# Another order of the prompt's query tiles, and a second buffer for the compression's chunk pairs

## The chip, the cores and the metric

One Trainium2 chip, one of its cores. The metric is the device time of one call in microseconds (us). Within one call the engines of a core run their own instruction streams side by side: PE (TensorE, matrix products), DVE (VectorE), ACT (ScalarE), POOL (GpSimd), and SP, which issues most of the transfers.

## The reference

One inference step of one layer of a hybrid decoder, for a prompt of 1024 tokens and 64 sample tokens (8 sequences of 8). The layer is a half feed-forward block, then a mixer in which attention and a Mamba-2 scan work side by side, then a second half feed-forward block. The change touches the attention alone:

```python
def nsa_mixer(q, q_pos, full_cmp, full_sel, o_win, gates, prm, slopes, sel_qb):
    kc = compress(full_cmp[:, :, 0], ...)          # 32-token blocks, stride 16, through a small MLP
    vc = compress(full_cmp[:, :, 1], ...)
    o_cmp, p_cmp = cmp_attention(q, q_pos, kc, vc, slopes)
    idx = select_blocks(p_cmp, q_pos, n_sel_blocks)
    o_sel = sel_attention(q, q_pos, idx, ...)
    g = jax.nn.sigmoid(gates)...
    return g[:, :, 0] * o_cmp + g[:, :, 1] * o_sel + g[:, :, 2] * o_win
```

For the prompt every query of tile t (128 queries) sees the keys of tiles 0 to t in the selected branch, the last 512 tokens in the window branch, and the compressed keys. For each of the 8 sample sequences a cache of 2048 tokens has to be compressed first, then its queries go through the same three branches.

## The kernel before

The kernel is one long program for one core, and a planner puts it in order: each engine gets a fixed list of instructions, made by simulating the program ahead of time. Whatever comes earlier in the program has precedence where several instructions are ready, an instruction is ready when its inputs are there and a buffer is free for its output, and a tile that is laid where older tiles were waits for the last use of those it overlaps.

The stage around the change is the prompt's attention. `for qi, qt in enumerate(KN["qt"])` (L1480) goes through the eight query tiles in the order of the tuple `qt` in the table `KN` (L37). Ahead of tile number qi it calls `compress_sample` as often as `cs[qi]` says, 3, 0, 2, 1, 1, 1, 0, 0 times, so that the eight sequences' compressions are in the program among the first six tiles. At qi 6 it also calls `mamba_setup`.

A query tile is worked off in two head groups of four heads. For each group, and for the selected (br 0) and the window branch (br 1): four heads' scores (L1549 to L1554: a matmul, a second one for the rest of the split, and masks), the maximum (DVE, L1559 to L1563), the exponential (ACT, L1565), sums and reciprocals (DVE, L1570 to L1572), and the multiplication of the four heads' probabilities by these (`scale`, L1576, on the engine that `KN["pb"][qi]` names letter by letter: a is ACT, L262, p is POOL, L264, v is DVE, L266). Then every 128 keys are one unit: four transposes into `pT` (L1587), one copy to `pt` (ACT and DVE in turn), and a matmul into `o` (L1596). Tile t has t+1 units of the selected branch, at most 5 of the window branch and one of the compressed keys in each group: 3 units for tile 0, 5, 7, 9, 11, 12, 13 and 14 for tiles 1 to 7. Between the scores of one head and its units nothing but these steps is needed; the next head, group or tile fills the waiting.

`compress_sample` (L1428) loads one sequence with an indirect transfer (`chk`, one buffer, L1430) and goes through it in eight chunk pairs: POOL and ACT each copy half a pair into `chp` (L1434), PE transposes it into `cT` (L1441, one bank, which the second product `c` of L1469 and L1472 shares), ACT makes `th` (L254), DVE makes `tl` (L1446), and 12 matmuls add to `cA` (L1462 to L1464). After four pairs come the activation `cxh` and the second product.

Once the attention's pools are closed, the program goes on with `sample_attention` and `mamba`. The first starts with a setup: some 15 index and constant tiles on POOL (`pi`, `hsel`, `G`, `E`, `bc`, `iw`, `tri`, `QS`, L1630 to L1722) and some 40 small instructions on DVE on them (L1633 to L1717, the greatest `bsel`, L1674). The pools of the new stage lie in the memory of the closed ones: those of `mamba`, with the chunk's tiles `xbc` that SP loads at L1255, grow from the left over the attention's keys, and those of `sample_attention` from the right over the attention's own tiles and then the compression's. Of a Mamba chunk the first steps are the transposes `xs_ps` (L1260), the DVE products `xdt` and `xde` (L1264, L1265) and the matmuls `ar` (L1282).

Of the kernel before, what the change touches and what calls it, by code (L numbers as in the profile page):

```python
# [9 lines left out]
F32 = mybir.dt.float32  # L10
# [7 lines left out]
P = 128  # L18
# [15 lines left out]
PAST = 2048  # L34
B0AT = (3, 5, 7, 9)
EARLY = {(0, 0): (0, 128), (1, 0): (640,), (0, 1): (), (1, 1): (768,)}
KN = {'Bt': 'a', 'cb': 'a', 'de': 'vv', 'ea': 'pp', 'st': 'p', 'hT': 'v', 'xm': 'p', 'yz': 'v', 'ysq': 'v', 'kT': 'aa', 'sPT': 'v', 'S': 'vv', 'ce': 'p', 'cm': 'p', 'pcT': 'v', 'msk': 'a', 'osb': 'av', 'q': 'sspss', 'pb': ['apppaapp', 'apppappp', 'apppappp', 'apvpappp', 'apppapvp', 'appvappp', 'vpvvvpvv', 'pvvvvvvv'], 'ph': ['aavaaa', 'aaaaaa', 'aaaaaa', 'aaaava', 'aaaaaa', 'aaaaaa', 'vavaaa', 'avaaaa'], 'pc': 'p', 'ob': 'aa', 'QA': 'aapv', 'QB': 'pv', 'chp': 'ap', 'th': 'aa', 'qt': (2, 7, 6, 5, 4, 3, 1, 0), 'cs': [3, 0, 2, 1, 1, 1, 0, 0], 'mix': [0, 0, 0, 0, 0, 0, 0, 0, 0]}  # L37
SLOPES = [2.0 ** -(h + 1) for h in range(NH)]


def f32(ap):
    return ap.bitcast(F32)
# [37 lines left out]
def hybrid_step(ctx: ExitStack, tc: tile.TileContext, *aps):  # L80
# [93 lines left out]
    def bankx(name):  # L174
        return PS.tile([P, 512], F32, name=name, tag="X", bufs=4)
# [17 lines left out]
    q = bankx("vec_ps")  # L193
# [669 lines left out]
    with pool("cv", bufs=2) as K:  # L863
# [40 lines left out]
        for group in [(0, 1)] + [(i,) for i in range(2, 8)]:  # L904
# [4 lines left out]
            if group[0] == 0:  # L909
                q = side("st_ps")  # L910
# [5 lines left out]
        for i in range(4):  # L916
            w = wcols(W, w_in, 1304 + P * i)
            zt = K.tile([P, T], F32, name="zt", tag="acc")
            for t0, n in WCHUNKS:
                q = bank("z")  # L920
# [5 lines left out]
        for z in range(2):  # L926
            q = side("cv_ps")
# [11 lines left out]
        for t0, n in WCHUNKS:  # L939
            q = bank("gd")  # L940
            dense(q, w, t0, n)
            nc.vector.tensor_tensor(gdT[:, t0:t0 + n], q[:32, :n], rms[:32, t0:t0 + n], op=OP.mult)
        q = side("gd_ps")
# [203 lines left out]
    for i in range(4):  # L1147
        w = wcols(W, w_in, P * i)
        for t0, n in WCHUNKS:
            q = bank("q")  # L1150
# [90 lines left out]
    def mamba(K, dt, dA, U, Us, Bof, bm, mU, mUs, nacs, dend, cdec, dsk):  # L1241
# [7 lines left out]
        for c in range(9):  # L1249
# [4 lines left out]
            xbc = K.tile([P, 8, P], F32, name="xbc")  # L1254
            QUEUES[KN["q"][0]].dma_start(xbc[:, :, :L], xbcD[:, :, ts].rearrange("i p t -> p i t"))  # L1255
            za = K.tile([P, 4, P], F32, name="za")
            QUEUES[KN["q"][1]].dma_start(za[:, :, :L], zD[:, :, ts].rearrange("i p t -> p i t"))
            q = b1("xs_ps")
# [10 lines left out]
            Bt = K.tile([P, 256], F32, name="Bt")  # L1269
            copy(KN["Bt"], Bt[:L], q[:L, :256])  # L1270
            cbp = b1("cb")
# [3 lines left out]
            cb = K.tile([P, 2, P], F32, name="cb")  # L1275
            copy(KN["cb"], cb[:L, :, :L], cbp[:L, :256].rearrange("p (g l) -> p g l", g=2)[:, :, :L])
            yp = b1("y")
            for g in range(2):
# [10 lines left out]
                for i in range(4):  # L1289
                    nc.scalar.activation(de[:L, i, :L], arv[:L, i, :L], AF.Exp,  # L1290
                                         bias=nacs[:L, c, 4 * g + i:4 * g + i + 1])
                sub(KN["de"][g], de[:L, :, :L], de[:L, :, :L], cb[:L, g:g + 1, :L].to_broadcast([L, 4, L]), OP.mult)
                sub(KN["ea"][g], ea[:, :, :L], ea[:, :, :L], xbc[:, 6 + g:7 + g, :L].to_broadcast([P, 4, L]), OP.mult)
                for i in range(4):
# [101 lines left out]
    CK = Ds.enter_context(pool("cmp", bufs=2))  # L1396
    PSC = Ds.enter_context(pool("cmp_ps", bufs=1, space=PSUM))
    with pool("att", bufs=2) as K, pool("att_ps2", bufs=3, space=PSUM) as PS2, \
# [29 lines left out]
        def compress_sample(b):  # L1428
            chk = CK.tile([P, 16, 2, 2, 64], F32, name="chk", bufs=1)
            nc.gpsimd.indirect_dma_start(  # L1430
                out=chk.rearrange("p s k g d -> p (s k g d)"), out_offset=None, in_=ch_cmp,
                in_offset=bass.IndirectOffsetOnAxis(ap=idx[:, b:b + 1], axis=0))
            def pairs(kv, jj):
                chp = CK.tile([P, 2, 2, 2, 64], F32, name="chp", bufs=1)  # L1434
                for g in range(2):
                    copy(KN["chp"][g], chp[:, :, g], chk[:, 4 * jj:4 * jj + 4, kv, g, :].rearrange(
                        "p (j r) d -> p j r d", r=2))
                q = b1("cT")
                for u in range(2):
                    for g in range(2):  # L1440
                        nc.tensor.transpose(q[:, P * (2 * u + g):P * (2 * u + g) + P],  # L1441
                                            chp[:, u, g].rearrange("p r d -> p (r d)"), ident)
                sv = q.rearrange("p (u c) -> p u c", u=2)
                th, tl = tpad[jj % 2]
                copy(KN["th"][jj % 2], th[:, :, :256], sv)
                nc.vector.tensor_tensor(tl[:, :, :256], sv, f32(th[:, :, :256]), op=OP.subtract)  # L1446

            steps = [(kv, jj) for kv in range(2) for jj in range(4)]
            pairs(*steps[0])
            for kv in range(2):  # L1450
                ab = PSC.tile([P, 2, P], F32, name="cA")
                for jj in range(4):
                    if (kv, jj) != steps[-1]:
                        pairs(*steps[4 * kv + jj + 1])
                    th, tl = tpad[jj % 2]
                    for u in range(2):
                        j = 2 * jj + u
                        for z in range(2):
                            wh, wl = w1h[:, kv, 8 * z + j], w1l[:, kv, 8 * z + j]
                            first = j == 0 and z == 0  # L1460
                            mh, ml = (x[:, u, z:z + 256].rearrange("p (g c) -> p g c", g=2) for x in (th, tl))
                            nc.tensor.matmul(ab, wh, mh, start=first, stop=False, skip_group_check=True)  # L1462
                            nc.tensor.matmul(ab, wl, mh, start=False, stop=False, skip_group_check=True)  # L1463
                            nc.tensor.matmul(ab, wh, ml, start=False, stop=(j == 7 and z == 1), skip_group_check=True)  # L1464
                hs = cmp_hidden(CK, ab[:, :, :127], None, kv, 127)
                q = b1("c2")
                for g in range(2):
                    if kv == 0:
                        nc.tensor.matmul(q[64 * g:64 * g + 64, :127], w2[:, 0], hs[:, g, :127],  # L1469
                                         start=True, stop=True)  # L1470
                    else:
                        nc.tensor.matmul(q[:127, 64 * g:64 * g + 64], hs[:, g, :127], w2[:, 1],  # L1472
                                         start=True, stop=True)
                if kv == 0:
                    nc.vector.tensor_copy(kcTs[:, b, :127], q[:, :127])
                else:
                    nc.vector.tensor_copy(vcs[:127, b, :], q[:127, :P])

        sequences = iter(range(8))
        for qi, qt in enumerate(KN["qt"]):  # L1480
# [5 lines left out]
            for g in range(2):  # L1486
                QA, QB = K.tile([P, 4, P], F32R, name="QA", bufs=2), QBq[g]
# [15 lines left out]
            for h in range(NH):  # L1503
                o = s[:, 64 * h:64 * h + 64]
                QA, QB = QAs[h // 4][:, h % 4], QBq[h // 4][:97, h % 4]
# [7 lines left out]
            pc = K.tile([P, NH, 64], F32, name="pc", bufs=1)  # L1513
# [12 lines left out]
            for g in range(2):  # L1526
                PT = {}
                for br in range(2):
# [6 lines left out]
                    for hh_ in range(4):  # L1535
                        pb = K.tile([P, 1024 if br == 0 else 640], F32, name=f"pb{br}", bufs=(5, 6)[br])
                        pbs.append(pb)
                        st, parts = 0, []
# [35 lines left out]
                    for hh_ in range(4):  # L1574
                        h, pb = 4 * g + hh_, pbs[hh_]
# [26 lines left out]
                ob = K.tile([P, 2, P], F32, name="ob", bufs=1)  # L1602
# [610 lines left out]
```

## Time and profile before

| | us |
|---|---|
| median of 3 runs | 2546.06 |
| lowest and highest of the 3 | 2540.13, 2546.14 |
| the profiled execution, its time | 2543.46 |
| its span, first to last instruction | 2541.8 |
| PE, DVE, ACT, POOL busy | 2449.2, 1751.7, 1092.3, 459.5 |

Times in the trace count from the start of the span. The engines' rows tell when an instruction began and how long it took; what stands in square brackets behind a row is how long the engine had been idle before, and what ended that. The two feed-forward blocks fill the span up to about 750 us and from about 1800 us on; the prompt's attention lies between about 1066 and 1485 us, and `sample_attention` and `mamba` run from there to about 1700 us.

### The profile page before, as it was taken

To read this page: it belongs to the slowest core of one execution; us is meant where nothing else is said; L and a number is where in the kernel's file an instruction comes from. 1 tells how busy PE (TensorE), PEld (TensorE's weight loads), DVE (VectorE), ACT (ScalarE), POOL (GpSimd) and SP (SyncE) were. 2 spreads that over 40 slices of the span, in tenths; PEclk is the share of its full clock that TensorE was granted. 3 is DMA by queue.
4 is the path that set the end of the run, shared out by engine and by line. 5 is a ranking of instruction groups with operands and counts; after the bars stand their busy time and mean duration, and the time that the engine had idled before them with its cause. 6 is when DMAs were issued, how large, how long until landed. Compare 5 with 4: busy or idle time off the path is not lost.

```text
span 2541.8 us, 48016 instructions
## 1 busy us (share of the span) xinstructions
PE 2449.2 (96%) x19111; PEld 2246.8 (88%) x19111; DVE 1751.7 (69%) x3601; ACT 1092.3 (43%) x2411; POOL 459.5 (18%) x545
## 2 busy tenths in 40 slices
PE   6999999999999999999999988999999999999998
PEld 6999999999999999867767755678999999999998
DVE  6767676677777546366667777656967676768776
ACT  7544444441143223166667644333544444443113
POOL 0000000011134213443334354431000000001110
PEclk9999999999999999999999989979999999999999
DMA  4334343598653223220010043543234444459654
GB/s 165 123 125 161 125 160 129 177 338 297 229 185 97 84 67 94 77 99 34 34 67 34 34 146 120 181 148 106 83 112 142 155 146 144 154 186 374 252 207 150
DMA packets 213563, 365.07 MB, mean 144 GB/s; under 512 B 17501, under 2 KB 130825, under 8 KB 211932
## 3 DMA queue, kind: packets, MB, share of 16 engines
q1 hardware_dynamic: 194408, 305.10, 34.8%
q0 software_dynamic: 7600, 38.59, 4.2%
q10 hardware_dynamic: 11332, 18.33, 2.1%
q8 instruction: 150, 2.46, 0.4%
q14 instruction: 73, 0.60, 0.1%
HBM read 246.39 MB, written 119.71 MB: 144 GB/s over the span
## 4 chain that ended last, share of the span: by engine, by line
PE 85%; DVE 8%; DMA 3%; ACT 3%; issue 1%; POOL 1%; SPq 0%; ACTq 0%; DVEq 0%; POOLq 0%
PE gY L352 6%; PE gY L353 6%; PE gY L351 6%; PE dq L609 6%; PE dq L608 5%; PE dq L610 5%; PE gX L352 5%; PE gX L353 5%; PE gX L351 5%; PE o L1596 3%; PE pT L1587 3%; PE s L1549 1%; PE cA L1462 1%; PE cA L1464 1%; PE cA L1463 1%
## 5 line engine op out<-in xcount | busy, mean ns | idle before, releaser
L609 PE MATMUL dq<-db,da 128*128 128x256 f32 (+1 forms) x1232 | 353.6, 288 | 0.3 <-DVE da L257 0.3
L610 PE MATMUL dq<-db,da 128*128 128x256 f32 (+1 forms) x1232 | 353.2, 288 | 0.0
L608 PE MATMUL dq<-db,da 128*128 128x256 f32 (+1 forms) x1232 | 349.6, 288 | 3.1 <-DMA db<-GD 1.9
L617 DVE TENSOR_TENSOR xT<-xT,dq 128x256 f32<-128x256 f32 (+1 forms) x456 | 187.1, 434 | 88.5 <-PE dq L610 86.8
L257 POOL TENSOR_TENSOR ds<-dw 128x512 f32<-128x512 f32 x22 | 29.0, 1318 | 1198.9 <-DMA dw<-in_ffn_wd_dram 515.6
L608 PEld LDWEIGHTS dq<-db,da 128*128 128x128 f32 x1232 | 230.4, 189 | 3.9 <-DVE xT L254 2.1
L610 PEld LDWEIGHTS dq<-db,da 128*128 128x128 f32 x1232 | 233.0, 189 | 0.0
L609 PEld LDWEIGHTS dq<-db,da 128*128 128x128 f32 x1232 | 232.0, 188 | 0.6 <-DVE da L257 0.5
L254 ACT CAST whi<-ws 128x512 fp32r<-128x512 f32 x156 | 96.5, 623 | 211.2 <-PE gY L353 145.2
L257 DVE TENSOR_TENSOR wlo<-raw,whi 128x512 fp32r<-128x512 f32 x164 | 113.8, 699 | 79.8 <-ACT whi L254 79.6
L254 ACT CAST da<-ds 128x512 fp32r<-128x512 f32 x88 | 52.7, 624 | 239.3 <-PE dq L610 93.4
L254 ACT CAST whi<-raw 128x512 fp32r<-128x512 f32 x176 | 109.0, 626 | 82.0 <-DMA raw<-in_w_out_dram 33.3
L257 DVE TENSOR_TENSOR wlo<-ws,whi 128x512 fp32r<-128x512 f32 x156 | 106.9, 689 | 42.0 <-ACT whi L254 39.2
L1565 ACT ACTIVATE pb<-s,mx 128x256 f32<-128x256 f32 (+3 forms) x192 | 105.2, 553 | 49.5 <-DVE mx L1563 33.0
L1587 PEld LDWEIGHTS pT<-ident,pb 128*128 128x128 f32 x528 | 59.4, 143 | 49.0 <-issue 41.5
L351 PE MATMUL gX<-B6h,whi 128*128 128x256 f32 (+1 forms) x320 | 91.4, 286 | 1.8 <-ACT Cc L358 1.8
L351 PE MATMUL gY<-B3h,whi 128*128 128x256 f32 (+1 forms) x320 | 91.5, 287 | 1.4 <-ACT whi L254 1.4
L352 PE MATMUL gX<-B6h,wlo 128*128 128x256 f32 (+1 forms) x320 | 91.8, 287 | 0.5 <-DVE wlo L257 0.5
L352 PE MATMUL gY<-B3h,wlo 128*128 128x256 f32 (+1 forms) x320 | 91.7, 287 | 0.2 <-DVE wlo L257 0.2
L352 PE MATMUL gY<-B2h,wlo 128*128 128x256 f32 (+1 forms) x320 | 91.8, 287 | 0.0
L352 PE MATMUL gX<-B7h,wlo 128*128 128x256 f32 (+1 forms) x320 | 91.7, 286 | 0.0
L351 PE MATMUL gX<-B7h,whi 128*128 128x256 f32 (+1 forms) x320 | 91.6, 286 | 0.0
(689 smaller groups left out, 8574.3 us busy)
## 6 DMA issues: line engine op xcount, KB each, us to landing
db<-GD SPq DMA_DIRECT2D x42, 1632.0 KB
GD<-Cc SPq DMA_DIRECT2D x154, 272.0 KB
GD<-his SPq DMA_DIRECT2D x84, 272.0 KB
raw<-in_ffn_wg_dram SPq DMA_DIRECT2D x22, 1024.0 KB
raw<-in_ffn_wu_dram SPq DMA_DIRECT2D x22, 1024.0 KB
dw<-in_ffn_wd_dram SPq DMA_DIRECT2D x44, 512.0 KB
GD<-hp SPq DMA_DIRECT2D x70, 272.0 KB
db<-GD SPq DMA_DIRECT2D x14, 1088.0 KB
```

Source lines behind the costliest of these rows:

```text
L254: return nc.scalar.copy(out, src) if eng == "a" else ENGINES[eng].tensor_copy(out, src)
L257: ENGINES[eng].tensor_tensor(out, x, y, op=op)
L351: nc.tensor.matmul(q, ah[:, k], b_, start=first, stop=False, skip_group_check=True)
L352: nc.tensor.matmul(q, al[:, k], b_, start=False, stop=False, skip_group_check=True)
L353: nc.tensor.matmul(q, ah[:, k], c_, start=False, stop=(k == 3), skip_group_check=True)
L608: nc.tensor.matmul(q, x, bh[:, u, o], start=first, stop=False, skip_group_check=True)
L609: nc.tensor.matmul(q, y, bh[:, u, o], start=False, stop=False, skip_group_check=True)
L610: nc.tensor.matmul(q, x, bl[:, u, o], start=False, stop=(u == np_ - 1), skip_group_check=True)
L617: nc.vector.tensor_tensor(x, x, q, op=OP.subtract if i == 4 else OP.add)
L1565: nc.scalar.activation(pb[:, st:st + pn], s, AF.Exp, bias=mx[:, 0:1], accum_out=part[:, hh_, i:i + 1])
L1587: nc.tensor.transpose(tq_[:kn, P * hh_:P * hh_ + P], src, ident)
L1596: mm = nc.tensor.matmul(O[64 * u:64 * u + 64], v_, p_, start=(ui < 2), skip_group_check=True, stop=(ui - len(held) + 1 + u >= len(units) - 2))
```

## The change

The tuple `qt` becomes 2, 7, 6, 0, 5, 1, 4, 3: the two smallest tiles move from the end to places four and six, and the last two tiles are 4 and 3. The lists of `pb` move with their tiles, so that each tile's probabilities are multiplied on the same engines as before, up to the letters' place. `cs` stays as it is, by position. The buffer `chp` of the compression has two slots in place of one; with that the pool of the attention's own tiles, which lies behind it, starts 2 KB per partition higher.

```diff
-KN = {... 'pb': ['apppaapp', 'apppappp', 'apppappp', 'apvpappp', 'apppapvp', 'appvappp', 'vpvvvpvv', 'pvvvvvvv'], ...
-      'qt': (2, 7, 6, 5, 4, 3, 1, 0), 'cs': [3, 0, 2, 1, 1, 1, 0, 0], ...}
+KN = {... 'pb': ['apppaapp', 'apppappp', 'apppappp', 'pvvvvvvv', 'apvpappp', 'vpvvvpvv', 'apppapvp', 'appvappp'], ...
+      'qt': (2, 7, 6, 0, 5, 1, 4, 3), 'cs': [3, 0, 2, 1, 1, 1, 0, 0], ...}
...
             def pairs(kv, jj):
-                chp = CK.tile([P, 2, 2, 2, 64], F32, name="chp", bufs=1)
+                chp = CK.tile([P, 2, 2, 2, 64], F32, name="chp", bufs=2)
```

## Rows read from the trace of the kernel before

**Rows 1.** The page's chain that ended last, its shares by engine.

```profile
PE 85%; DVE 8%; DMA 3%; ACT 3%; issue 1%; POOL 1%; SPq 0%; ACTq 0%; DVEq 0%; POOLq 0%
```

**Rows 2.** Busy time of the engines in stretches of the span: from A to B, its length, then busy us (and instructions) of PE, PE's weight loads, DVE, ACT and POOL, the granted clock of PE, the DMA engines' share, GB/s.

```profile
1102.00:1474.00 372.00, 366.07 (x2517) 267.54 (x2515) 246.34 (x587) 247.66 (x667) 140.61 (x211) 1.00 0.11 41
1474.00:1492.00 18.00, 9.88 (x31) 4.92 (x31) 17.12 (x70) 2.98 (x8) 15.92 (x17) 0.61 0.92 306
...
1440.00:1474.00 34.00, 34.00 (x255) 26.40 (x253) 25.91 (x79) 22.48 (x76) 9.84 (x22) 1.00 0.00 1
```

**Rows 3.** PE's instructions in order of time around the end of the attention: start, us, engine, line, what, count, idle time before.

```profile
1470.04 0.28 PE L1464 MATMUL cA<-tl,w1h 128*128 128x256 f32 x1
...
1472.10 1.07 PE L1596 MATMUL o<-pt,VAc 64*64 64x512 f32 x2
...
1473.77 0.23 PE L1554 MATMUL s<-mdiag,identb 128*128 128x128 bf16 x1
...
1477.57 0.33 PE L1587 MATMUL pT<-ident,pb 128*128 128x128 f32 x1 [3.13 <-DVE pb L266]
...
1481.31 1.97 PE L1596 MATMUL o<-pt,VA 128*64 128x512 f32 x4 [1.70 <-DVE pt L254]
1483.22 1.97 PE L1596 MATMUL o<-pt,VAc 64*64 64x512 f32 x2
1485.11 1.11 PE L1260 MATMUL xs_ps<-ident,xbc 128*128 128x128 f32 x4
...
1491.64 2.08 PE L1282 MATMUL ar<-U,dA 128*128 128x128 f32 x8 [3.28 <-DVE xde L1265]
```

**Rows 4.** The chain that ended last, from 1469 to 1499 us: start, us, what.

```profile
1475.43 0.05 DVE ti L1633
...
1477.45 1.63 DVE pb L266 x3
...
1480.66 0.60 DVE pt L254
...
1483.82 2.29 DVE bsel L1674
...
1488.88 0.42 DVE qT L1607
...
1490.38 0.60 DVE xdt L1264
1490.98 0.61 DVE xde L1265
```

**Rows 5.** POOL's instructions in order of time: a tile's multiplications, the last of the attention, and the first of the setup.

```profile
1414.44 3.04 POOL L264 TENSOR_TENSOR pb<-pb,sm 128x512 f32<-128x512 f32 x3 [1.17 <-DVE sm L1572]
...
1470.27 0.40 POOL L264 TENSOR_TENSOR pb<-pb,sm 128x128 f32<-128x128 f32 x1 [5.90 <-DVE sm L1572]
1470.63 0.17 POOL L1630 IOTA pi<- 128x1 int32 x1
```

**Rows 6.** SP's issues in order of time.

```profile
1473.96 0.39 SPq L1255 DMA_DIRECT2D xbc<-xbcD  x1
```

**Rows 7.** The timelines of PE, ACT, DVE and POOL, their lines of the compression: two pairs that follow one another closely, and two between which POOL's copy came late.

```profile
1194.63 0.61 PE L1441 MATMUL cT<-ident,chp 128*128 128x128 f32 x4
1195.75 0.41 ACT L254 COPY chp<-chk 128x256 f32<-128x256 f32 x1
1195.89 0.69 DVE L1446 TENSOR_TENSOR tl<-cT,th 128x512 fp32r<-128x512 f32 x1 [0.28 <-ACT th L254]
1197.32 0.61 PE L1441 MATMUL cT<-ident,chp 128*128 128x128 f32 x4
...
1261.80 0.60 PE L1441 MATMUL cT<-ident,chp 128*128 128x128 f32 x4
1265.44 0.39 POOL L254 COPY chp<-chk 128x256 f32<-128x256 f32 x1
1270.14 0.60 PE L1441 MATMUL cT<-ident,chp 128*128 128x128 f32 x4
```

**Rows 8.** The first transposes of the first and of the last sequence, from PE's timeline.

```profile
1102.86 0.60 PE L1441 MATMUL cT<-ident,chp 128*128 128x128 f32 x4
...
1428.06 0.60 PE L1441 MATMUL cT<-ident,chp 128*128 128x128 f32 x4
```

**Rows 9.** Groups of instructions by line and shape in the attention: line, engine, operation, out<-in, shapes, count, then busy us and mean ns of one, then idle time before and its releasers. The last row is from 1475 to 1497 us, the others from 1100 us on.

```profile
L1565 ACT ACTIVATE pb<-s,mx 128x512 f32<-128x512 f32 x40 | 27.3, 686 | 7.0 <-DVE mx L1563 4.5 <-DVE mx L1559 1.7 <-PE pT L1587 0.6
L1559 DVE TENSOR_REDUCE mx<-s 128x1 f32<-128x512 f32 x16 | 10.5, 685 | 1.1 <-PE s L1554 1.0
L266 DVE TENSOR_SCALAR pb<-pb,sm 128x128 f32<-128x128 f32 x14 | 4.8, 396 | 0.1
L266 DVE TENSOR_SCALAR pb<-pb,sm 128x128 f32<-128x128 f32 x4 | 2.0, 564 | 0.0
```

**Rows 10.** Busy time in stretches early in the attention, before the first transposes of the compression; columns as in rows 2.

```profile
1075.00:1080.00 5.00, 4.57 (x14) 2.94 (x14) 3.35 (x8) 4.34 (x12) 5.00 (x5) 0.50 1.09 410
1080.00:1085.00 5.00, 3.71 (x17) 2.21 (x15) 4.27 (x11) 3.86 (x13) 4.74 (x10) 0.79 0.99 342
1085.00:1090.00 5.00, 4.49 (x17) 2.52 (x17) 1.94 (x5) 3.48 (x10) 3.80 (x5) 0.55 0.60 166
1090.00:1095.00 5.00, 4.84 (x27) 3.24 (x26) 2.70 (x7) 2.72 (x8) 2.45 (x5) 0.77 0.76 324
```

More of the change, by code (lines that the diff above doesn't have):

```diff
@@ L36 @@
 EARLY = {(0, 0): (0, 128), (1, 0): (640,), (0, 1): (), (1, 1): (768,)}
-KN = {'Bt': 'a', 'cb': 'a', 'de': 'vv', 'ea': 'pp', 'st': 'p', 'hT': 'v', 'xm': 'p', 'yz': 'v', 'ysq': 'v', 'kT': 'aa', 'sPT': 'v', 'S': 'vv', 'ce': 'p', 'cm': 'p', 'pcT': 'v', 'msk': 'a', 'osb': 'av', 'q': 'sspss', 'pb': ['apppaapp', 'apppappp', 'apppappp', 'apvpappp', 'apppapvp', 'appvappp', 'vpvvvpvv', 'pvvvvvvv'], 'ph': ['aavaaa', 'aaaaaa', 'aaaaaa', 'aaaava', 'aaaaaa', 'aaaaaa', 'vavaaa', 'avaaaa'], 'pc': 'p', 'ob': 'aa', 'QA': 'aapv', 'QB': 'pv', 'chp': 'ap', 'th': 'aa', 'qt': (2, 7, 6, 5, 4, 3, 1, 0), 'cs': [3, 0, 2, 1, 1, 1, 0, 0], 'mix': [0, 0, 0, 0, 0, 0, 0, 0, 0]}
+KN = {'Bt': 'a', 'cb': 'a', 'de': 'vv', 'ea': 'pp', 'st': 'p', 'hT': 'v', 'xm': 'p', 'yz': 'v', 'ysq': 'v', 'kT': 'aa', 'sPT': 'v', 'S': 'vv', 'ce': 'p', 'cm': 'p', 'pcT': 'v', 'msk': 'a', 'osb': 'av', 'q': 'sspss', 'pb': ['apppaapp', 'apppappp', 'apppappp', 'pvvvvvvv', 'apvpappp', 'vpvvvpvv', 'apppapvp', 'appvappp'], 'ph': ['aavaaa', 'aaaaaa', 'aaaaaa', 'aaaava', 'aaaaaa', 'aaaaaa', 'vavaaa', 'avaaaa'], 'pc': 'p', 'ob': 'aa', 'QA': 'aapv', 'QB': 'pv', 'chp': 'ap', 'th': 'aa', 'qt': (2, 7, 6, 0, 5, 1, 4, 3), 'cs': [3, 0, 2, 1, 1, 1, 0, 0], 'mix': [0, 0, 0, 0, 0, 0, 0, 0, 0]}
 SLOPES = [2.0 ** -(h + 1) for h in range(NH)]
```

## The prediction

> **What bounds the kernel now.** I read the page's chain first: it goes through PE for 85% of the span and through DVE for 8% [rows 1], so a change can only save where PE stands still, runs at half its clock, or where the chain leaves it. Then I cut the attention into stretches. From 1102 to 1474 us PE is busy for 366.07 of 372 us at full clock [rows 2]: 5.9 us to be had there in all, and whatever is put in another order inside it keeps its sum. From 1474 to 1492 us the picture turns over: PE 9.88 of 18 us, at a mean clock of 0.61, and DVE 17.12 of 18 [rows 2]. The loss is in these 18 us, and the change bears on what runs there.
>
> The third view, PE's timeline, shows what they consist of. The last scores of tile 0 end at about 1474.0 us; then PE waits 3.13 us for DVE's multiplications and 1.70 us for a copy, does its last four and two matmuls into `o` in 1.97 us each where the group before took 1.07, transposes Mamba's first chunk at 1485.11 and waits 3.28 us for `xde` before `ar` at 1491.64 [rows 3]. The fourth view, the chain, says why: from 1475.43 to 1491.64 us, 16.2 us, it lies nearly all on DVE. Of that the attention and Mamba own `pb` 1.63, `pt` 0.60, `qT` 0.42, `xdt` 0.60 and `xde` 0.61 [rows 4], 3.9 us together; the other 12.3 us, with `bsel` alone 2.29 [rows 4], are the setup of the sample attention and small steps. The setup stands in front of the attention's last steps and of Mamba's first.
>
> Why doesn't it run sooner? POOL makes its first index tile at 1470.63 us, directly behind its last multiplication; before that multiplication POOL had been idle for 5.90 us and did not take it [rows 5]. PE issues the compression's last product at 1470.04 us [rows 3]. By the sizes in the code the setup's tiles lie over the compression's weights and buffers, and I take the end of the compression for what lets them in. So a second chain matters: the compression of eight sequences, whose first transposes are at 1102.86 us for the first and at 1428.06 for the last [rows 8], 325.2/7 = 46.5 us for each. It ends only 3.7 us before the last scores do (1473.77 less 1470.04, rows 3), which is why the setup has nothing to hide behind.
>
> **Part 1: the second `chp` buffer.** It adds no instruction. With one slot the copies for a pair wait for the transposes of the pair before, with two they may be done one pair ahead, and the gather of the next sequence, which waits for the last copies, may be issued that much sooner. What it saves depends on what spaces the pairs. In a close pair, transposes at 1194.63 and 1197.32 us, ACT's copy is there at 1196.16 and `tl` leaves the bank `cT` at 1196.58 [rows 7]: there the bank decides, and the second buffer saves nothing. In a wide one, transposes at 1261.80 us, POOL's copy starts at 1265.44, 3.0 us after they end, behind other POOL work [rows 7]; there up to 3.0 us go. By my count of the timeline about ten pairs of 64 are like that, mostly less late. Ends: nothing, and ten times 3.0, 30 us, for all eight sequences; I take 12, nearer to the close pair, which is the usual one. PE is full meanwhile, so these microseconds are no gain by themselves: the compression's share of PE comes sooner and the tiles' later.
>
> **Part 2: the order.** The same 148 units (2 groups of 3, 5, 7, 9, 11, 12, 13 and 14) are worked off; only the place of tiles 0 and 1 and the two last tiles change. Tiles 0 and 1 with their short chains go to where PE has compression and tiles 5 and 4 to fill with; their waits (3.13 and 1.70 us now) are covered there by the score matmuls of the next tile. If that cover failed they would stand inside the full stretch, as much as now, 4.8 us. I cost this at nothing, with ends of 4.8 us lost and, since 5.9 us are idle there now, 3 gained.
>
> The end is now tile 3's. *Old end:* 3.13 + 1.70 us idle, and half clock: two `o` groups at 1.97 in place of 1.07, 1.8 us, and some 0.5 on the transposes; 7.1 us. *New end,* from tile 3's last score: maximum 0.69 and exponential 0.69 [rows 9], about 0.4 of small steps, then POOL's three multiplications of 512 columns, 3.04 us in that tile now [rows 5], together 4.8 us before the window branch's units can start. To cover that PE has, at best, the four units of the selected branch: a unit is four transposes, at most 0.61 us as those of the compression [rows 7], I take 0.5 behind one another, and about 0.25 of the 1.07 us of four `o` [rows 3]: 0.75 us, four of them 3.0. So PE idles 1.8 us at the least and 4.8 if those units are done already. Behind it come five units at 0.75, where only the last copy and pair, about 0.6 us, is bare. New end: 2.4 to 5.4, and up to 2.3 more if the clock falls as it does now; I take 5.2. Part 2 saves 7.1 − 5.2 = **1.9 us**, between −0.6 and 4.7.
>
> SP is moved too: it can issue `xbc` when the last scores have read the keys, 1473.96 us now, right behind the score at 1473.77 [rows 3, 6]. With tile 3 that issue has more matmuls behind it than with tile 0, so the load stays hidden. `mamba_setup` goes from tile 1 to tile 4, further from the end; it is hidden by PE's fullness in both places.
>
> **Part 3: the setup.** With the compression ending 12 us sooner, and the last scores about 3 us sooner (tile 3 leaves more PE work behind them), its lead over the last scores grows from 3.7 to about 13 us. In that lead DVE has its idle share: 1 − 25.91/34 = 24% in the last 34 us, 34% over the whole attention [rows 2]. So 3.1 to 4.4 us of DVE's setup leave the 12.3 on the chain; I take **4.0**. Ends: 0 (no lead), and 9 (the lead is long; what remains of the 18 us is about the 9.2 us that the new end needs anyway: 4.8, five units at 0.75 and 0.6).
>
> **Sum.** −1.9 − 4.0 = −5.9 us, against the profiled execution 2543.46 − 5.9 = 2537.6. That execution lies 2.6 us under the median of the three runs; carried to the median, 2546.06 − 5.9 = **2540.2 us**. What follows the attention is moved sooner as a whole; I allow 3 us either way for where its transfers and clock falls come to lie.
>
> **Rivals.** *The setup is hidden whole.* The compression ends 25 us or more ahead (30 saved, the upper end of part 1). Then 9 us go from the setup and 3 from the end: 2546.1 − 12 = 2534. For it: 9 of the 12.3 us have no other reason to be there. Against: DVE's idle share of 24% fills slowly.
>
> *The buffer does nothing.* If `cT` and its sharing with `c` space nearly all pairs, as in the close one [rows 7], the compression ends where it does and the setup stays behind it; only the end's 1.9 us are left: 2544.
>
> *POOL and DVE hold each other up.* Four multiplications of 128 columns on DVE took 0.564 us each beside the busy POOL of the last 22 us, 0.396 in the mean of the attention [rows 9]. The setup moved under tile 3 would meet that tile's POOL multiplications; stretched by that ratio, 1.42, the 3.04 us become 4.3 and the 4.0 us saved 2.8: −5.9 + 1.3 + 1.2 = −3.4, 2542.7. The Trainium skill, SBUF — State Buffer, section "Who interferes with whom", says that GpSimd and certain VectorE instructions take turns on a shared pair of ports, and that the second to come blocks wholly until the first is done. By that rule a held-up instruction would lose whole multiplications rather than a ratio; the two rows bear out a loss, not its form.
>
> *The filler runs out (slower).* When the compression ends, tiles 4 and 3 are alone on PE. Before the first compression transposes, from 1075 to 1095 us, the attention alone leaves PE idle for 2.39 of 20 us, 12%, though at reduced clock and beside heavy transfers [rows 10]. Tiles 4 and 3 have 40 of 148 units; PE's 366 us less about 123 for the compression (8 times 96 matmuls and 32 transposes, at 0.12 each by the same estimate) give 243/148 = 1.6 us for a unit, 66 us for both. If the compression ended a whole 50 us ahead, 12% of that, 6 us, would eat the saving; with all 66 us bare, 8 us, a fallen clock and small tiles not covered (4.8) it would be 2546.1 + 8 + 2.3 + 4.8 − 7 = 2554. It decides against the change from some 50 us of lead on, or less if the bare tiles let the clock fall.
>
> **How the numbers follow.** About 0.3%, 7.6 us, is what a measurement of this kernel can tell from no change: faster means under 2538.4, slower over 2553.7. My forecast (2540.2, its own range 2533 to 2546) has 0.45, of which 0.17 lie past the bound; the setup hidden whole 0.19, all faster; the buffer that does nothing 0.17 and the held ports 0.06, all within; the filler 0.13, of which 0.10 are slower than the bound, for clock falls that it may add behind. Faster 0.36, same 0.54, slower 0.10. The range from 2529 to 2550 takes in the first four cases and the milder half of the last.
>
> **What would show it.** The compression's last `cA` should come 8 to 20 us before the last scores, and POOL's `pi` right behind it; if `pi` still waits for the attention's end, the memory was not the reason. In the 18 us after the last scores DVE should be below 80% and `ar` come some 6 us sooner, counted from the last scores with PE's work evened out. PE's wait for the multiplications should now name POOL and be 2 to 5 us. If PE's idle time before the last scores is well over 5.9 us, or its clock falls there, the filler rival holds; and if the attention ends sooner but the whole time does not follow, the later stage has given it back.

## The result and the profile after

The changed kernel takes 2565.91 us, median of 4 runs (2563.09 to 2567.87), beside 2544.24 of the kernel before in the same 4 rounds: 1.0087 times as long, 95% interval 1.007 to 1.0104. The prediction said 2540.2, at most 2550. It is wrong in sign and outside its range.

The profiled execution took 2567.87 us, its span 2566.1. I cut both spans at the same five marks: the compression's first product `cA`, the last score product of the last tile (the one with `KB`), the start of the last two matmuls into `o`, the first `ar`, and the end. The stretches add up to the span, so a difference can be put in its place. Before: 1105.1, 368.6, 9.6, 8.4 and 1050.2 us. After: 1105.1, 382.4, 16.8, 6.2 and 1055.6. So 13.8 us are lost ahead of the last scores, 5.0 between these and `ar`, and 5.4 behind it.

The page's chain by engine, as in [rows 1]: PE's share fell, those of DVE, DMA and ACT grew.

```profile
PE 81%; DVE 9%; DMA 4%; ACT 4%; issue 2%; POOL 1%; SPq 0%; ACTq 0%; DVEq 0%; POOLq 0%
```

Busy time in stretches of the kernel after (columns as in rows 2): first `cA` to last score, from there to `ar`, and the stretch that answers to the last of [rows 2].

```profile
1105.10:1487.49 382.39, 361.87 (x2435) 260.97 (x2433) 257.04 (x632) 238.80 (x644) 140.11 (x211) 0.98 0.11 39
1487.49:1510.52 23.03, 19.03 (x96) 9.54 (x94) 9.52 (x27) 9.25 (x22) 13.99 (x16) 0.91 0.84 268
1440.00:1474.00 34.00, 26.75 (x145) 15.78 (x144) 28.36 (x75) 15.18 (x37) 12.05 (x21) 0.90 0.00 1
```

The same stretches of the kernel before.

```profile
1105.09:1473.65 368.56, 362.63 (x2493) 264.82 (x2492) 244.19 (x583) 244.30 (x657) 139.86 (x210) 1.00 0.11 41
1473.65:1491.64 17.99, 9.87 (x35) 4.91 (x34) 16.91 (x69) 3.30 (x9) 15.92 (x17) 0.62 0.90 299
```

Between 1440 and 1474 us PE was full before and now works 26.75 of 34 us, at a clock of 0.90. Up to the last scores it stands still for 20.5 us (382.39 less 361.87) where it stood 5.9.

PE's timeline, first the first transposes of the first and the last sequence [rows 8], then the end of the compression and of the attention [rows 3].

```profile
1102.87 0.60 PE L1441 MATMUL cT<-ident,chp 128*128 128x128 f32 x4
1407.06 0.94 PE L1441 MATMUL cT<-ident,chp 128*128 128x128 f32 x4
...
1446.07 0.28 PE L1464 MATMUL cA<-tl,w1h 128*128 128x256 f32 x1
...
1459.13 1.98 PE L1596 MATMUL o<-pt,VA 128*64 128x512 f32 x4 [4.38 <-DVE pt L254]
...
1487.72 0.23 PE L1554 MATMUL s<-mdiag,identb 128*128 128x128 bf16 x1
...
1504.32 1.07 PE L1596 MATMUL o<-pt,VAc 64*64 64x512 f32 x2
...
1510.52 1.70 PE L1282 MATMUL ar<-U,dA 128*128 128x128 f32 x7
```

A sequence's compression takes (1407.06 − 1102.87)/7 = 43.5 us in place of 46.5, and the last `cA` comes 24.0 us sooner. It now leads the last scores by 41.4 us, where the prediction took 13; some 15 of the 41.4 are the lateness of the scores themselves, since in e4 and e8 below, where they come on time, the lead is 26.1. The waits that the prediction counted at the end are gone; in their place PE waits 4.38 us at 1459, for a copy that DVE makes late. POOL's and DVE's timelines there say why.

```profile
1450.52 1.50 POOL L264 TENSOR_TENSOR pb<-pb,sm 128x640 f32<-128x640 f32 x1
1451.98 0.13 POOL L1630 IOTA pi<- 128x1 int32 x1
...
1456.33 1.28 POOL L1700 TENSOR_SCALAR_AFFINE_SELECT tri<-tri 128x961 f32<-128x961 f32 x1
...
1452.33 0.23 DVE L1717 TENSOR_SCALAR idx<-idx 128x8 int32<-128x8 int32 x1
...
1452.41 5.25 DVE L1717 TENSOR_SCALAR idx<-idx 128x8 int32<-128x8 int32 x3
...
1457.80 0.68 DVE L1559 TENSOR_REDUCE mx<-s 128x1 f32<-128x512 f32 x1
1458.40 0.67 DVE L254 COPY pt<-pT 128x512 f32<-128x512 f32 x1
```

With the compression over, the setup of the sample attention comes in at once: `pi` at 1451.98, directly behind POOL's multiplication, 36 us ahead of the last scores where it was 3 us ahead [rows 3, 5]. POOL then makes its constants one after another until 1457.9. Of DVE's small `idx` instructions the first took 0.23; the next three, from 1452.41 on, are not through until 1457.66, nor is anything behind them in DVE's list, where the last tile's maximum and copy stand.

### The profile page after: what moved, and what is told of

Same layout as the page of the kernel before. It is cut to its first block, busy times and chain, and to the rows that moved or that the text cites. A ratio compares the mean times of both kernels' runs of the same rounds, so it can differ in the third digit from the quotient of the medians.

```text
span 2566.1 us, 48032 instructions
## 1 busy us (share of the span) xinstructions
PE 2461.5 (96%) x19111; PEld 2248.1 (88%) x19111; DVE 1754.7 (68%) x3601; ACT 1091.8 (43%) x2411; POOL 459.5 (18%) x545
## 4 chain that ended last, share of the span: by engine, by line
PE 81%; DVE 9%; DMA 4%; ACT 4%; issue 2%; POOL 1%; SPq 0%; ACTq 0%; DVEq 0%; POOLq 0%
PE gY L352 6%; PE gY L353 6%; PE gY L351 6%; PE dq L609 5%; PE dq L608 5%; PE dq L610 5%; PE gX L352 4%; PE gX L353 4%; PE gX L351 4%; PE o L1596 3%; PE pT L1587 2%; PE s L1549 1%; PE xbc L237 1%; PE xbc L239 1%; PE cA L1462 1%
## 5 line engine op out<-in xcount | busy, mean ns | idle before, releaser
L264 POOL TENSOR_TENSOR pb<-pb,sm 128x640 f32<-128x640 f32 (+7 forms) x70 | 84.5, 1231 | 50.9 <-DVE sm L1572 42.7
L1549 PE MATMUL s<-KA,QA 128*128 128x256 f32 (+3 forms) x192 | 79.5, 414 | 14.2 <-ACT pb L1565 12.9
L353 PE MATMUL gX<-B6l,whi 128*128 128x256 f32 (+1 forms) x320 | 92.2, 288 | 0.0
```

Source lines behind the costliest of these rows:

```text
L353: nc.tensor.matmul(q, ah[:, k], c_, start=False, stop=(k == 3), skip_group_check=True)
L1549: nc.tensor.matmul(s, QAs[g][:, hh_], KA[:, br, g, kk], start=True, stop=False, skip_group_check=True)
```

## The experiments

All stretches below are cut at the same marks; one profiled execution each, the median from 4 to 8 runs, and the ratio to the kernel before in the same rounds (its medians were 2541.4 to 2544.1; the table has that of the rounds with the changed kernel).

| run | median | ratio, 95% interval | first cA at | to last scores | to last o | to ar | to the end |
|---|---|---|---|---|---|---|---|
| before | 2544.24 | | 1105.1 | 368.6 | 9.6 | 8.4 | 1050.2 |
| after | 2565.91 | 1.0087, 1.007 to 1.0104 | 1105.1 | 382.4 | 16.8 | 6.2 | 1055.6 |
| e1 | 2561.38 | 1.0067, 1.0043 to 1.0091 | 1104.3 | 369.6 | 21.4 | 8.4 | 1055.5 |
| e2 | 2566.85 | 1.0089, 1.0071 to 1.0107 | 1107.0 | 393.8 | 7.5 | 7.7 | 1050.4 |
| e4 | 2585.12 | 1.0163, 1.0146 to 1.018 | 1107.6 | 366.9 | 15.8 | 8.8 | 1088.4 |
| e5 | 2556.21 | 1.0048, 1.003 to 1.0065 | 1101.8 | 368.6 | 8.0 | 8.0 | 1065.5 |
| e6 | 2556.15 | 1.0057, 1.004 to 1.0074 | 1099.9 | 369.2 | 25.7 | 7.8 | 1048.6 |
| e7 | 2568.42 | 1.0082, 1.0054 to 1.0109 | 1105.1 | 390.4 | 12.5 | 5.4 | 1056.1 |
| e8 | 2562.26 | 1.0071, 1.0047 to 1.0095 | 1100.4 | 367.5 | 26.4 | 6.8 | 1053.7 |
| e9 | 2556.11 | 1.0046, 1.003 to 1.0062 | 1102.9 | 364.5 | 11.2 | 11.0 | 1064.5 |
| e10 | 2552.68 | 1.0046, 1.0024 to 1.0068 | 1102.9 | 372.1 | 17.8 | 7.7 | 1048.7 |
| e11 | 2554.73 | 1.0052, 1.0036 to 1.0068 | 1105.2 | 372.1 | 17.8 | 6.7 | 1051.1 |
| e12 | 2565.26 | 1.0087, 1.0055 to 1.0118 | 1107.7 | 386.5 | 13.1 | 6.3 | 1049.0 |
| e13 | 2551.19 | 1.0042, 1.0026 to 1.0059 | 1105.8 | 368.6 | 7.7 | 10.7 | 1057.4 |
| e14 | 2561.08 | 1.0082, 1.0059 to 1.0105 | 1098.2 | 382.2 | 16.3 | 6.3 | 1053.7 |
| e15 | 2558.18 | 1.007, 1.0053 to 1.0087 | 1105.9 | 369.7 | 23.4 | 6.3 | 1052.1 |

The work ahead of the first `cA` is the same in all of them; it differs by up to 9.5 us between executions, so a few us of a profiled time say nothing of the change.

**Each part alone.** e1 is the changed kernel with one buffer:

```diff
-                chp = CK.tile([P, 2, 2, 2, 64], F32, name="chp", bufs=2)
+                chp = CK.tile([P, 2, 2, 2, 64], F32, name="chp", bufs=1)
```

> The new order of tiles with one buffer for the chunk pairs, as before. Theories: FILLER (two buffers let the compression finish some 40 us ahead of the last scores, and the last tile, alone on PE, leaves gaps and half clock), SETUP (the compression's early end lets the sampled attention's setup in, and its DVE and POOL work comes ahead of the last tile's chain), ORDER (the small tiles in the middle, or the large one at the end, cost by themselves). Against the kernel before (2544 us): FILLER and SETUP both give 2537 to 2548, since the compression then ends with the attention; ORDER gives 2555 to 2568.

e2 is the kernel before with two:

```diff
-                chp = CK.tile([P, 2, 2, 2, 64], F32, name="chp", bufs=1)
+                chp = CK.tile([P, 2, 2, 2, 64], F32, name="chp", bufs=2)
```

> The old order of tiles (1 and 0 last) with two buffers for the chunk pairs. FILLER: the compression ends some 24 us sooner and the small tiles, whose chains are shorter, are alone at the end: 2555 to 2568. SETUP: the setup comes early too, beside small tiles that need DVE less: 2545 to 2560. ORDER: 2535 to 2546, and the attention's end at 1485 us or sooner.

Each part alone is slower, by 18 and 23 us, and both together by 22: they don't add up. In e1 the time is ORDER's. By the marks the last scores come on time and the loss lies behind them (29.8 us to `ar` against 18.0) and behind `ar`. But a mark says when, not how much is done: tile 3 leaves more of PE's work behind its last scores. PE's own loss in e1 lies ahead of them: it stands idle there for 9.1 us, and the granted clock is 0.50 for 13.7, where before it was idle for 5.9 and the clock never fell. Behind the scores its idle time is 9.0 us, and was 8.1. The whole setup lies there too, and e1's timelines of DVE and PE show the hold-up of the changed kernel again.

```profile
1481.39 3.97 DVE L1717 TENSOR_SCALAR idx<-idx 128x8 int32<-128x8 int32 x2 [0.41 <-POOL E L1659]
...
1481.95 3.42 DVE L254 COPY pt<-pT 128x512 f32<-128x512 f32 x1
...
1485.49 1.14 PE L1596 MATMUL o<-pt,VA 128*64 128x512 f32 x4 [3.12 <-DVE pcol L1657]
```

In e2 the loss lies wholly ahead of the last scores, +25 us: FILLER's numbers.

**The setup held back.** e4 is the changed kernel with the setup's DVE and POOL instructions behind the attention's last `qT` sum and last POOL multiplication; e5 the same with the kernel before.

```diff
+        with tc.issue_after(last_v.ins), tc.issue_after(last_p.ins):
+            pi = SC.tile([P, 1], I32, name="pi")
...
```

> The changed kernel with the instructions of the setup on DVE and POOL put behind the attention's last ones on these engines. SETUP: the last tile's gaps close, the attention ends 12 to 20 us sooner than in the changed kernel (1505 us in its trace), the setup then costs 5 to 10 us behind it, and the time is 2550 to 2560. FILLER: the attention ends within 5 us of the changed kernel's, the setup adds 4 to 10 us: 2566 to 2576. ORDER: as FILLER.

A window of e4: the last tile alone, from the last `cA` to the last score.

```profile
1448.40:1474.47 26.07, 24.72 (x140) 13.84 (x139) 20.62 (x42) 17.60 (x44) 9.65 (x9) 1.00 0.00 1
```

PE is busy for 95% of it at full clock, without filler and without setup, and the last `o` comes at 1490.3 us where it came at 1504.3: SETUP's mechanism, in the new order. The sum did not follow, because 38 us are then lost behind `ar`, far more than the 5 to 10 I gave it. e5 asks whether that is the price of a late setup in general.

> The kernel before with the setup's instructions on DVE and POOL behind the attention's last ones: a control for the run that held them in the changed kernel. There the attention's last scores came as early as before (366.9 us after the first cA, against 382.4 in the changed kernel and 368.6 before), but the time from the first ar to the end grew from 1055.6 to 1088.4 us. LATE SETUP (that growth is the price of a setup that starts behind the attention, whatever the order): here too 15 to 35 us are lost behind ar: 2558 to 2580. OTHER (the growth belongs to the new order or the second buffer): within 5 us of before.

It is, in kind: 15.4 us behind `ar`, with 2.0 saved ahead of it; the median is just under the range given. The 38 of e4 contain more that this control doesn't explain.

**The compression held back.** e6 puts the eighth sequence behind the last tile's `s_cmp` product (`cs` 3, 0, 2, 1, 1, 0, 0, 1).

```diff
+            for _ in range(KN["cs"][qi] if qi >= 7 else 0):
+                with tc.issue_after(sc_mm.ins):
+                    compress_sample(next(sequences))
```

> The changed kernel with the compression's eighth sequence put behind the last tile's s_cmp product, so that its products fall among the last tile's. FILLER and SETUP: the compression ends with the attention again, PE is busy over 97% up to the last scores, and the time is 2535 to 2547. ORDER: 2555 to 2568. If FILLER alone is right and not SETUP, the gain over the changed kernel is that of this run and the run with the setup held has none.

By the time it is ORDER's case, 10 us better than the changed kernel and 12 worse than before. Again the scores come on time (369.2), with the end of the compression and the whole setup left for the tail, which takes 25.7 us to the last `o`; and again PE has lost ahead of them, 14.4 us idle against 5.9, so the busy share of 97% that FILLER and SETUP asked for isn't reached.

**The setup's DVE part held to the last scores.** POOL's part may run as soon as the memory is free. e7 with the old order and two buffers, e8 with the changed kernel.

```diff
-                            nc.vector.tensor_reduce(mx[:, 0:1], ...
+                            last_mx = nc.vector.tensor_reduce(mx[:, 0:1], ...
...
+        with tc.issue_after(last_mx.ins):
+...
```

> The kernel before with two buffers for the chunk pairs and the setup's DVE instructions put behind the maximum of the last scores, about where they ran before; POOL's own may run as soon as the memory is free. SETUP (all that the second buffer costs, +25 us up to the last scores, is the setup's DVE work that it lets in ahead of the attention): first cA to last score 366 to 372 us, total 2538 to 2548. FILLER (the small tiles are alone on PE when the compression is over): 380 us or more, total 2556 to 2566. POOL (its iotas alone hold DVE up): 375 to 382.

> The changed kernel with the setup's DVE instructions put behind the maximum of the last scores; POOL's may run as soon as the memory is free. SETUP: first cA to last score 366 to 371 us in place of 382.4; what is left against before is the tail of the last tile, 16 to 22 us from the last scores to the last product o in place of 9.6: total 2550 to 2560. FILLER: 378 to 384 us up to the last score, total 2563 to 2572. POOL alone: about 375, total 2556 to 2564.

They part the two orders. In e8 the last scores are on time (367.5): POOL's iotas alone, run at 1447.7 to 1452.1, cost nothing there; the tail grew to 26.4, since the setup is now in it, and the time is above SETUP's range. In e7 the last scores are as late as in e2, with the setup away. Windows of e7, when the small tiles are alone:

```profile
1464.00:1468.00 4.00, 1.79 (x13) 1.24 (x11) 4.00 (x9) 1.02 (x4) 3.49 (x8) 1.00 0.00 0
1468.00:1472.00 4.00, 3.37 (x17) 3.27 (x18) 3.93 (x9) 2.16 (x8) 2.73 (x4) 0.60 0.01 4
1472.00:1476.00 4.00, 3.35 (x18) 2.84 (x16) 3.12 (x10) 1.96 (x6) 1.54 (x4) 0.50 0.00 0
```

PE stands still for 2.21 of the first 4 us; from some 1469 us on the granted clock is 0.50, the lower level of 1.2 GHz, and stays there for 17 us. So FILLER holds for tiles 1 and 0, and SETUP for tile 3.

**Where the small tile stands.** e9 moves tile 0 alone (order 2, 7, 6, 0, 5, 4, 3, 1, one buffer, the `pb` lists with their tiles).

> The kernel before (one buffer) with tile 0 alone moved to the middle: 2, 7, 6, 0, 5, 4, 3, 1. TAIL (a large last tile costs 7 to 16 us behind the last scores, a small one in the middle nothing): the tail from the last scores to the last o is 9 to 13 us, and the time 2541 to 2550. MIDDLE (a small tile among the large ones costs by itself): the stretch from the first cA to the last scores grows by 4 us or more, 2550 to 2560.

Tail and middle are as TAIL says: 364.5 us to the last scores, the shortest of all runs, and 386.6 to `ar`, as before. The time is above TAIL's range all the same: the 14.3 us that it loses lie behind `ar`, where neither theory put them. The compression ends last there, so the setup is late.

**The dose.** e10 is the kernel before with a second buffer for the last four sequences only; e11 and e12 are e9 with it for the last four and five.

```diff
-                chp = CK.tile([P, 2, 2, 2, 64], F32, name="chp", bufs=1)
+                nm = "chq" if b >= 4 and jj % 2 else "chp"
+                chp = CK.tile([P, 2, 2, 2, 64], F32, name=nm, bufs=1)
```

> The kernel before, in its old order, with the second buffer for the chunk pairs in the last four sequences alone, so that the compression ends only a part of the 24 us sooner, about by the 8 to 13 us of lead that the prediction reckoned with. DOSE (a small lead lets the setup in without emptying the filler): the last scores come within 2 us of before's 368.6 us after the first cA, the time from there to ar shrinks from 18 to 13 to 17 us, total 2537 to 2545. STEEP (small tiles lose as soon as the filler is gone, for each us of lead about one): first cA to last scores 374 to 382, total 2548 to 2558.

> The order 2, 7, 6, 0, 5, 4, 3, 1 (with one buffer it reached the last scores 364.5 us after the first cA, against 368.6 before, and lost 14 us behind ar, where the setup had begun only 11 us before ar, against 21 before) with the second buffer in the last four sequences alone, so that the compression ends shortly ahead of the last scores. LATE SETUP (the loss behind ar comes from the setup's late start): first cA to ar 383 to 390 us, ar to end 1047 to 1056, total 2536 to 2546. OTHER (the loss behind ar belongs to this order): ar to end 1060 or more, total 2550 to 2560.

> As the run before it, with the second buffer in the last five sequences, so that the compression is over well ahead of the last scores and tile 1 is alone for a while. STEEP: first cA to last scores 372 us or more, total 2548 to 2560. DOSE: 364 to 368 us, total 2534 to 2544.

e10 comes nearest to the prediction's own case, with a lead of 7.6 us in place of 3.6, and it loses 11 us up to `ar`: STEEP, though less ahead of the scores (372.1) and more behind them. PE's and DVE's timelines of e10 behind the last score:

```profile
1475.19 0.33 PE L1555 MATMUL s<-mdiag,identb 128*128 128x128 bf16 x1
...
1487.09 0.44 PE L1588 MATMUL pT<-ident,pb 128*128 128x128 f32 x1 [6.72 <-DVE pb L266]
...
1474.82 0.45 DVE L1663 TENSOR_SCALAR E<-E,pcol 64x512 f32<-64x512 f32 x1
...
1479.98 3.80 DVE L1709 COPY QS<-qT 64x64 f32<-64x64 f32 x8
...
1486.67 0.87 DVE L266 TENSOR_SCALAR pb<-pb,sm 128x128 f32<-128x128 f32 x4
```

The setup has got in front of the last group's multiplications in DVE's list, and PE's wait for these grows from 3.13 us [rows 3] to 6.72. In e11 the setup is sooner than in e9, and what e9 lost behind `ar` is back (1051.1 for 1064.5), as LATE SETUP says; but the stretch to `ar` is 10 us longer, as in e10, not the 383 to 390 expected from the first `cA`, and the time is in OTHER's range. e12, with 26.5 us of lead, loses another 9 up to `ar`, and its time is above STEEP's range. The timelines of POOL, DVE and PE, first e9, then e11:

```profile
1478.56 0.13 POOL L1630 IOTA pi<- 128x1 int32 x1 [6.98 <-PE cA L1463]
1485.76 2.27 DVE L1674 TENSOR_TENSOR bsel<-bc,bs 128x2048 f32<-128x2048 f32 x1
1489.50 2.27 PE L1282 MATMUL ar<-U,dA 128*128 128x128 f32 x16
```

```profile
1472.77 0.23 POOL L1631 IOTA pi<- 128x1 int32 x1
1484.60 2.27 DVE L1675 TENSOR_TENSOR bsel<-bc,bs 128x2048 f32<-128x2048 f32 x1
1501.86 1.92 PE L1282 MATMUL ar<-U,dA 128*128 128x128 f32 x8
```

**What in the setup costs.** e13 (on before) and e14 (on after) take `bsel` to POOL and the copies of `QS` to ACT; e15 is the changed kernel with the setup's DVE part behind the eighth maximum of the last tile's first group.

```diff
-        nc.vector.tensor_tensor(bsel, ...
+        nc.gpsimd.tensor_tensor(bsel, ...
-            nc.vector.tensor_copy(QSv[...
+            nc.scalar.copy(QSv[...
```

```diff
+                            if qi == 7 and g == 0 and br == 1:
+                                last_mx = mx_
```

> The kernel before with two parts of the setup taken off DVE: the sum for bsel (2.29 us on DVE) to POOL, the eight copies of QS to ACT. DVE TIME (DVE's share of the setup stands between the attention's last products and the first ar): the time from the last scores to ar shrinks from 18.0 to 13 to 16 us, ar to end unchanged (1047 to 1054), total 2536 to 2542. HIDDEN (that work lies beside other waits): within 1.5 us of 18, total 2541 to 2547. COLLIDE (the two engines run into each other, or bsel comes late from POOL): 2547 or more.

> The changed kernel with the same edit: bsel's sum on POOL, the copies of QS on ACT, some 4 us less of DVE work among the last tile's chain. DVE TIME (the 15 us that the early setup adds up to the last scores are DVE's busy time, about one for one): first cA to last scores 376 to 379 in place of 382.4, total 2556 to 2562. BLOCK (they come from the five microseconds in which DVE stands beside POOL's iotas and the half clock that follows): 381 to 384, total 2562 to 2568.

> The changed kernel with the setup's DVE instructions put behind the eighth maximum of the last tile, some ten microseconds later than they came, when POOL's iotas are over; all of them still run ahead of the last scores or beside them. BLOCK: no DVE instruction of 5 us, no gap of 4.4 us and no half clock behind it: first cA to last scores 372 to 377 in place of 382.4, ar 4 to 8 us sooner, total 2556 to 2562. DVE TIME: the same work waits in the same chain, only later: the tail grows by what the scores gain, first cA to ar within 2 us of 405.4, total 2563 to 2568.

e15 separates it. Its windows from the first `cA` to the last score and on to `ar`:

```profile
1105.87:1475.58 369.71, 357.47 (x2435) 259.93 (x2434) 244.45 (x614) 237.78 (x642) 138.59 (x209) 1.00 0.11 41
1475.58:1505.27 29.69, 22.40 (x96) 10.66 (x94) 17.61 (x46) 10.36 (x23) 16.07 (x17) 0.79 0.68 209
```

The 5 us on DVE and the gap of 4.38 are gone, the last scores come 12.7 us sooner after the first `cA`, and `ar` 6.0 sooner (399.4 for 405.4); the median falls by 7.7. That is BLOCK's range for the time; but 6.7 of the 12.7 come back between the scores and `ar`, as DVE TIME has it for part of the cost. e14 keeps the 5.25 us and is as late at the last scores as the changed kernel (382.2): BLOCK again, though its time is a little under BLOCK's range, and it does not rule out DVE's time, since its sum for `bsel` on POOL held DVE up anew (`bwin` 3.53 us). e13 shows the same on the kernel before (18.3 us to `ar`, HIDDEN, but 2551 us in all, COLLIDE):

```profile
1481.40 4.23 POOL L1674 TENSOR_TENSOR bsel<-bc,bs 128x2048 f32<-128x2048 f32 x1 [4.50 <-DVE bs L1673]
...
1482.09 4.09 DVE L1685 SCALAR_TENSOR_TENSOR bwin<-iw,slope,bwin 128x512 f32<-128x512 f32 x1
```

`bwin` took about 0.75 us elsewhere (1487.38 to 1488.13 in the kernel before). No version that ran beats the kernel before.

## Why the prediction was wrong

*What bounds the kernel* was right, with the consequence that I did not take seriously enough: PE was full up to the last scores [rows 2], so nothing could be won there and all of it could be lost.

*Part 1* named the right effect. The last `cA` comes 24.0 us sooner where it took 12, but the order has a share in that. From the first `cA` to the last it is 364.95 us before, 351.24 with the buffer alone (e2), 371.31 with the order alone (e1), and 340.97 with both. So in the old order the buffer is worth 13.7 us, nearly the 12, and in the new one 30.3, its upper end. What the part left out is that the buffer can cost something inside the full stretch: in e2 PE is idle for 12.2 us while the compression runs, where it was 5.9. That the end of the compression lets the setup in was right too: `pi` follows it in every run where it ends early.

*Part 2* holds for the last tile's own waits, and was not what failed. Counted as the prediction did, up to the end of the last `o`: before, PE waits 4.83 us behind the last scores, and the lower clock takes 2.7 more (half of what PE was busy at 0.50), 7.5 in all; after, it waits four times for 0.34 or 0.35 us and the lower clock takes 1.7, 3.1 in all; with the setup held back (e4) it is 1.9. So the new end saved 4 to 6, not 1.9. In the middle tile 0 costs little: in e9 PE is idle for 7.0 us ahead of the last scores, and the clock is 0.50 for 3.4 us. The order alone, with one buffer, costs more ahead of the last scores than the 4.8 us that the part allowed: 3.2 more of idle time, and 6.6 by the clock (e1). That the stretch to the last `o` is longer by 7 us is mostly work that PE did ahead of the scores before: it is busy for 19.0 of the 23.0 us, and was for 9.9 of 18.0. SP issues `xbc` at 1487.91, right behind the last score [rows 6]; the load stayed hidden.

*Part 3 is the step that failed*: "So 3.1 to 4.4 us of DVE's setup leave the 12.3 on the chain; I take 4.0. Ends: 0 (no lead), and 9". It has the wrong sign. The setup did leave the end (6.2 us from the last `o` to `ar`, 8.4 before), and took more than that elsewhere. I gave the setup the idle share of DVE, 24%, as if it were free to use. But DVE works through a fixed list, and each tile's chain passes through DVE at the maximum, the sums, a part of the multiplications and every second copy; a setup instruction in that list delays all of these, whatever DVE's mean share. Beside PE's full stretch this shows at once. The runs size it. From the first `cA` to `ar` it is 386.6 us before, and in the new order with two buffers 391.6 with the setup held back (e4), 399.4 with its DVE part let in without the hold-up (e15), and 405.4 as the change has it. By these single executions the new order and the second buffer cost 5.0 (with a part of the setup still ahead of `ar` in e4), the setup's instructions in the last tile's list 7.8, and the 5 us hold-up with what follows 6.0: together 18.9. This is the stretch up to `ar` alone: e4 loses more behind it than it wins here, so no run shows the whole time without this cost. e10 shows the same in the old order with only 4 us more of lead: 11 us lost, a wait of 6.72 for 3.13.

*The rivals.* "POOL and DVE hold each other up" was right in kind and too small: I stretched multiplications by 1.42, for 2.5 us; measured were one hold-up of 5.25 on DVE and 6.0 us in all. The Trainium skill, SBUF — State Buffer, section "Who interferes with whom", says that the second to come blocks wholly; by that rule a whole instruction would be lost rather than a ratio, and the trace agrees with the form (a 0.23 us kind of instruction took 5 us), only that DVE waited here through a whole run of POOL's instructions, of which the rows show none longer than 1.5. "The filler runs out" was taken to decide from 50 us of lead; with tiles 1 and 0 at the end it costs 13 to 14 us at leads of 39 and 43 (e7, e2): while they are alone PE is idle for 4.6 us in both, and the clock is 0.50 for 17 and 20 us. Alone at the end, tile 3 costs 1.4 us (e4). By the prediction's own sign, PE's idle time well over 5.9 us ahead of the last scores (20.5), this rival would have held; e4 and e8 show that in this order it was the setup. "The setup is hidden whole" had its condition fulfilled (25 us ahead) and the opposite result. "The buffer does nothing" fell.

*Behind `ar`* I allowed 3 us either way; the change lost 5.4. One thing goes with a long stretch: when `bsel` begins less than 4 us before `ar`, or after it (e9, e5, e4), that stretch takes 1064 us or more, and otherwise 1048.6 to 1057.4. In e9 and e5 a small DVE instruction of the sample attention stands for 5.6 and 4.1 us there, beside a run of POOL's; how much of the loss that makes is not shown. The changed kernel is not such a case. The order of PE's instructions behind the first Mamba transposes differs between these kernels; whether that makes 1055.6 of 1050.2, or 1088 in e4, stays open.

The longer tails of e1 and e6, where the compression ends behind the last scores, are in the main work that PE had left: to `ar` it is busy for 20.9 of 29.8 us in e1 and 25.3 of 33.5 in e6, and was for 9.9 of 18.0. *Left open* besides is what makes PE lose 10 and 12 us more than before ahead of the scores there, by idle time and clock.

## What to carry to other kernels

When an engine is full, an edit that speeds up the work beside it gains nothing there, and changes what comes next: ask which stage the freed memory lets in, and into whose instruction lists. Idle time of an engine that works in a fixed order is no slack for new work if every step of the bounding chain passes through it; what counts is where in its list the new instructions land. And work that fills the gaps of short chains is worth most when the short chains are last: finishing it early takes away its cover.

## What the runs showed of the hardware

A DVE instruction that met POOL's back-to-back run waited for far more than one instruction of it: 5.25 us for three `idx` of 128x8, beside ten POOL instructions of 0.13 to 1.28 us, from `E` to `tri`. Not every DVE instruction is held. In e8 the same POOL run left DVE's maxima (0.68 us) and copies out of `pT` (0.68 us) as they were. Those that were held beside POOL lie between tiles of SBUF, but that alone doesn't decide it: in e2 a `ti` of 128x1 took 0.14 us beside POOL's iota `iw` of 0.57. In e13 a pair of products `de` took 6.82 us, beside four POOL instructions behind one another (1499.75 to 1505.41), where the two took 0.87 and 0.69 in the kernel before.

```profile
1499.74 6.82 DVE L257 TENSOR_TENSOR de<-de,cb 128x512 f32<-128x512 f32 x2 [0.98 <-ACT de L1290]
...
1499.75 1.06 POOL L257 TENSOR_TENSOR st<-st,cdec 128x512 f32<-128x512 f32 x1
1500.75 2.49 POOL L257 TENSOR_TENSOR ea<-ea,xbc 128x512 f32<-128x512 f32 x2
1503.20 2.21 POOL L257 TENSOR_TENSOR ce<-ce,tri 128x961 f32<-128x961 f32 x1
```
